# Scan differences as stick-breaking weights, and dilated blocks handled in pairs, in a two-layer hybrid attention trunk

## The chip, the cores and the metric

The kernel runs on one core of one Trainium2 chip. The metric is the device time of one execution in microseconds (us), lower is better. Three executions of the kernel before took 3222.48, 3223.91 and 3230.89 us, with a median of 3223.91 us. A core has several engines that run their own instruction streams side by side: TensorE (PE, matrix products and transposes; its weight loads are listed as PEld), VectorE (DVE), ScalarE (ACT), GpSimd (POOL) and SyncE (SP, which issues DMAs). They meet through semaphores.

## The reference, cut to what matters

Two layers, each with one input projection, two token mixers that read its outputs, SiLU gates, and one output projection. 2048 tokens, 4 stick-breaking heads and 12 dilated heads of 64 numbers each. Numbers are float32.

```python
# stick-breaking, for a block of 128 queries and the keys up to it
z = einsum('bhqd,bhkd->bhqk', qblk, k[:lk]) / 8
ls_z = log_sigmoid(z)
log_surv = where(mask, ls_z - z, 0)          # log(1 - sigmoid(z)), mask: key < query
acc = (sum of log_surv over the keys after this one)
a = where(mask, exp(ls_z + acc), 0)          # sigmoid(z[k]) * product over later keys of (1 - sigmoid(z))
o = einsum('bhqk,bhkd->bhqd', a, v[:lk])

# dilated window, three patterns (window, dilation): (128,1), (512,4), (2048,16)
# tokens r apart form a sequence; blocks of 128 queries see their own and the previous 128 keys
s = einsum('brnqhd,brnkhd->brnhqk', qb, kk) / 8     # kk: previous block and own block
# per pattern: softmax with its maximum and its sum; the three outputs are mixed by their denominators
```

## The kernel before, in words

A layer runs in three stretches: the projection with the gate path (until about 787 us in the first layer), the stick-breaking mixer `_stick` with the tail of the projection's stores (until about 1016 us), then the dilated mixer `_dilated`, whose last weights are interleaved with the output projection `_output` (until about 1613 us). The second layer repeats this. PE instructions of the mixers are pinned to the order in which the code issues them (`pin`); the other engines' orders are made by a scheduler when the program is built.

**Stick.** The work of a layer is 80 units: a pair of heads, a block of 128 queries, and up to 512 keys. `front(u)` makes the scores of both heads (two fp32r products per head, L541 and L542, and a mask product L544 in diagonal blocks), ACT takes sigmoid(-z) (L549, the survival factors g) and sigmoid(z) (L550), DVE runs a product scan over the keys (L551, into r, whose first entry carries over to the next unit of the block), and POOL multiplies sigmoid(z) by the scan (L557). `mid(u)` transposes the weights on PE (L570) and copies them out of PSUM (L572, ACT for head 0, DVE for head 1). `back(u)` makes the value products (L584). The loop issues `front(u+2)`, `mid(u)`, and after every second unit two `back`s in a row (`LEAD, BATCH = 2, 2`).

**Dilated.** Six pairs of heads, and for each 48 groups: 16 query blocks in each of the three patterns p = 0, 1, 2. A block has one key block if it is in pattern 0 (whose own and previous block share one window) or first in its sequence (4 of 16 in p = 1, 1 of 16 in p = 2), 21 of 48 in all; the others have two. `front(g)` makes four score products of 256 columns (L732: two heads, two halves of the precision split), also where only 128 columns are used; DVE adds the mask and takes the minimum (L734), ACT takes the exponential (L738). `mid(g)` transposes (L753, four or two times) and copies (L755, DVE for odd g, ACT for even g). Every fourth group `back` makes the value products of four groups (L767). The softmax statistics of a pair are brought together while the next pair runs: `stats_b` puts two sets of PE products (L802 to L807) into two banks of the ring `w_r`, ACT copies them (L810), and a chain of small DVE, POOL and ACT steps (L815 to L826, with a DVE reciprocal L822) makes the weights. `weigh` broadcasts the weights of one block with one PE product (L837) into a bank of `w_r`, and DVE multiplies the outputs by it (L838), 16 times per pair, one per group from the fifteenth group on. The last pair's weighs run in the tail, between output projection products (L932, L935, L936).

PSUM has eight banks: in `_dilated` the scores use 0, 1, 2, the transposes 3, 4, the value products 5, and `w_r` 6, 7. The loop issues one group per step: `front(g+3)`, `mid(g)`, every fourth step `back`, then statistics or one `weigh`.

Of the kernel before, what the change touches and what calls it, by code (L numbers as in the profile page):

```python
# [459 lines left out]
def _stick(tc, mem, sb_scr, g_scr, mix, ident, ident_r):  # L460
    nc = tc.nc
# [14 lines left out]
    wk1 = mem.get("G1", [128, 12, 512])  # L476
    r_s = Slices([wk0[:, i] for i in range(6)])
    gam = Slices([wk0[:, 6 + i] for i in range(6)])
    b_s = Slices([wk1[:, i] for i in range(6)])
    at_s = Slices([wk1[:, 6 + i] for i in range(6)])  # L480
    nc.gpsimd.memset(wk0[:, 6:12, 512:513], 1.0)
    qs_, ks1, ks2, vn, gt = {}, {}, {}, {}, {}
# [49 lines left out]
    def front(u):  # L532
# [14 lines left out]
        for h, z in enumerate(zs):  # L547
            b, g, r = b_s.get(), gam.get(), r_s.get()
            nc.scalar.activation(g[:, 512 - n:512], z[:, :n], AF.Sigmoid, scale=-0.125)  # L549
            nc.scalar.activation(b[:, :n], z[:, :n], AF.Sigmoid, scale=0.125)  # L550
            nc.vector.tensor_tensor_scan(  # L551
                out=r[:, 0:n + 1][:, ::-1], data0=g[:, 512 - n:513][:, ::-1],
                data1=z[:, 0:1].to_broadcast([128, n + 1]),
                initial=1.0 if top else carry[h][:, 0:1],
                op0=ALU.mult, op1=ALU.bypass)
            carry[h] = r
            nc.gpsimd.tensor_tensor(out=b[:, :n], in0=b[:, :n], in1=r[:, 1:n + 1], op=ALU.mult)  # L557
            prod[u].append(b)
# [4 lines left out]
    def mid(u):  # L563
        pr, i, lo, hi = units[u]
        n = hi - lo
        ats[u] = []
        for h, b in enumerate(prod.pop(u)):
            ps = t_r.get([128, 512])
            for j in range(n // 128):
                pin(nc.tensor.transpose(ps[:, 128 * j:128 * j + 128], b[:, 128 * j:128 * j + 128], ident))  # L570
            at = at_s.get()
            (nc.vector.tensor_copy if h else nc.scalar.copy)(at[:, :n], ps[:, :n])  # L572
            ats[u].append(at)
# [20 lines left out]
    todo = []  # L594
    LEAD, BATCH = 2, 2
    load(1)
# [20 lines left out]
def _dilated(tc, mem, v_scr, qk_scr, g_scr, mix, masks, sel, ident, neg1):  # L617
# [3 lines left out]
    nc.sync.dma_start(out=mk, in_=masks)  # L621
    s_r = mem.bank_ring(0, 1, 2)
    t_r = mem.bank_ring(3, 4)
    o_r = mem.bank_ring(5)
    w_r = mem.bank_ring(6, 7)
    pa, pb = mem.get("H0", [128, 2, 2, 256]), mem.get("H1", [128, 2, 2, 256])
    pe_s = Slices([pa[:, 0], pa[:, 1], pb[:, 0], pb[:, 1]])
    ta, tb = mem.get("H6", [128, 2, 2, 2, 128]), mem.get("H7", [128, 1024])
    td = mem.get("H5", [128, 2, 2, 2, 128])
    ts_s = Slices([td[:, 0], td[:, 1], ta[:, 0], ta[:, 1], tb[:, 0:512].rearrange("p (c h q) -> p c h q", c=2, h=2)])  # L630
# [74 lines left out]
    def front(g):  # L705
# [5 lines left out]
        c, n, first = geom(p, b)  # L711
        u0 = 0
        if p == 0:
            w0 = min(b, 14) * 128
            u0 = 128 * b - w0
        else:
            run, stp = (32, 4) if p == 1 else (8, 1)
            w0 = 0 if first else run * (n - 1)
        un = 128 if first else 256
        m0 = M_OWN[p] + 128 - un  # L720
        sc = s_r.get([128, 2, 256])
        pe = pe_s.get()
        for h in range(2):
            qb = qq[pr][h][p].bitcast(F32R)[:, 128 * b:128 * b + 128]
            for s in range(2):
                kt = kk[pr][h][s]
                if p == 0:
                    kv = kt[:, w0:w0 + 256]
                else:
                    kv = kt.rearrange("p (c a) -> p c a", c=NT)[  # L730
                        :, c::stp, w0:w0 + 2 * run].rearrange("p c (w a) -> p w c a", w=2)
                pin(nc.tensor.matmul(sc[:, h], qb, kv, start=s == 0, stop=s == 1))  # L732
        for h in range(2):
            nc.vector.tensor_tensor_reduce(  # L734
                out=pe[:, h, :un], in0=sc[:, h, u0:u0 + un], in1=mk[:, m0:m0 + un],
                scale=-0.125, scalar=3.0e38, op0=ALU.add, op1=ALU.min,
# [7 lines left out]
    def mid(g):  # L744
# [9 lines left out]
        ts = ts_s.get()  # L754
        (nc.vector.tensor_copy if g % 2 else nc.scalar.copy)(ts[:, :nch], tp[:, :nch])  # L755
        tss[g] = ts
# [39 lines left out]
    def stats_b(pr, eng):  # L796
# [15 lines left out]
        ll = sm[:, 1]  # L812
        mn = tb[0:32, 896:1024]
        ew = tb[0:32, 512:896].rearrange("p (q a) -> p q a", q=3)
        nc.vector.tensor_tensor(out=mn, in0=nm[:, 0], in1=nm[:, 1], op=ALU.min)  # L815
# [41 lines left out]
    for g in range(LEAD):  # L857
        front(g)
    for g in range(total):
        pr, t = g // 48, g % 48  # L860
# [4 lines left out]
        if pr + 1 < NPAIR:  # L865
# [4 lines left out]
            if t == 36:  # L870
                make_q(pr + 1, 1)
        if g + LEAD < total:
            front(g + LEAD)
        mid(g)
        if g % 4 == 0 and g:
            back(g - 4)
        if pr:
            if t == 1:
                stats_a(pr - 1, nc.gpsimd)
            elif t == 5:  # L880
                stats_b(pr - 1, nc.gpsimd)
            elif 15 <= t < 31:
                weigh(pr - 1, t - 15)
                if t % 4 == 2:
                    gate(pr - 1, (t - 15) // 4)
        yield
# [95 lines left out]
```

## Time and profile before

| | us |
|---|---|
| three executions | 3222.48, 3223.91, 3230.89 |
| median | 3223.91 |
| profiled execution | 3228.57 |
| its span on the core | 3226.8 |
| PE busy in it | 3137.9 (97%) |
| DVE busy | 1648.3 (51%) |
| ACT busy | 1534.4 (48%) |
| POOL busy | 1234.4 (38%) |

Busy times of PE overlap a little and their ends are modelled, since products are pipelined, so a PE that is 97% busy may still have gaps. The pace of PE is better read from the starts of successive groups of instructions in the timeline. The granted clock of PE was 0.99 to 1.00 of full speed (2.4 GHz) in all stretches shown below. The table hides that stages differ: in the projection PE alone is the limit, while in the mixers several engines take turns.

### The profile page before, as it was taken

Reading aid. Unit: us, or ns where it says so; the run is one execution under the profiler, and the core shown is the slowest. Engines: PE = TensorE matmul, PEld = TensorE weight load, DVE = VectorE, ACT = ScalarE, POOL = GpSimd, SP = SyncE. Lnnn points to the kernel's source line nnn. Section 1 sums busy time; section 2 is a strip of 40 time slices with the busy share of each in tenths; the row PEclk is TensorE's granted clock in tenths of the full one; section 3 lists DMA queues with packets and bytes.
Section 4 is the critical chain, followed back from the end, with each engine's and each line's share of the span. In section 5 each row is a group of like instructions: output and inputs, shape, how many; then the busy total and the mean of one; then the engine's idle time right before and its main releaser. Section 6 shows DMA issues by size and latency. Waiting matters only on the chain.

```text
span 3226.8 us, 59494 instructions
## 1 busy us (share of the span) xinstructions
PE 3137.9 (97%) x21968; PEld 2683.2 (83%) x21968; DVE 1648.3 (51%) x4147; ACT 1534.4 (48%) x4317; POOL 1234.4 (38%) x1302
## 2 busy tenths in 40 slices
PE   8999999999999999989999999999999999999899
PEld 8888888887777999878898888888877789988787
DVE  6134440015988777764141444301169887777721
ACT  5123331114878998962031233211158789988510
POOL 1067751102664444451010677511036734444500
PEclk9999999999999999999999999999999999999999
DMA  5123346317023556454442233463160235663443
GB/s 198 63 73 113 112 138 181 122 48 204 15 83 93 165 155 193 117 164 150 128 135 72 70 113 105 149 189 104 59 186 21 83 106 151 178 187 100 140 145 108
DMA packets 324066, 396.40 MB, mean 123 GB/s; under 512 B 20160, under 2 KB 270016, under 8 KB 313536
## 3 DMA queue, kind: packets, MB, share of 16 engines
q1 hardware_dynamic: 323776, 392.60, 40.0%
q8 instruction: 174, 2.85, 0.4%
q14 instruction: 116, 0.95, 0.1%
HBM read 235.24 MB, written 148.90 MB: 119 GB/s over the span
## 4 chain that ended last, share of the span: by engine, by line
PE 81%; DVE 5%; ACT 4%; POOL 4%; issue 3%; DMA 2%; SPq 0%; POOLq 0%; ACTq 0%; DVEq 0%
PE b L310 11%; PE b L311 11%; PE b L309 11%; PE b L732 7%; PE b L767 5%; PE b L753 5%; PE b L451 4%; PE b L453 4%; PE b L452 4%; PE b L935 4%; PE b L936 4%; PE b L932 3%; PE b L584 3%; PE b L367 2%; ACT H L738 2%
## 5 line engine op out<-in xcount | busy, mean ns | idle before, releaser
L738 ACT ACTIVATE H<-H,T 128x256 f32<-128x256 f32 (+1 forms) x1152 | 522.7, 457 | 45.9 <-DVE T L734 43.4
L311 PE MATMUL b<-F,F 128*128 128x512 f32 (+1 forms) x1344 | 484.1, 360 | 0.4 <-DVE F L282 0.3
L734 DVE CUSTOM_DVE_ANT_0 H<-b,M 128x256 f32<-128x256 f32 (+1 forms) x1152 | 368.6, 361 | 168.9 <-PE b L732 66.2
L732 PE MATMUL b<-F,F 128*128 128x256 f32 x2304 | 412.3, 303 | 0.3 <-DVE T L734 0.3
L557 POOL TENSOR_TENSOR G<-G,G 128x512 f32<-128x512 f32 (+3 forms) x320 | 320.5, 1017 | 228.5 <-DVE G L551 171.6
L551 DVE TENSOR_TENSOR_SCAN G<-G,b 128x513 f32<-128x513 f32 (+3 forms) x320 | 336.5, 1085 | 33.0 <-ACT G L550 32.7
L732 PEld LDWEIGHTS b<-F,F 128*128 128x128 f32 x2304 | 326.4, 190 | 20.1 <-issue 19.5
L310 PE MATMUL b<-F,G 128*128 128x512 f32 (+1 forms) x896 | 324.7, 362 | 0.0
L309 PE MATMUL b<-F,G 128*128 128x512 f32 (+1 forms) x896 | 324.3, 362 | 0.0
L310 PE MATMUL b<-F,F 128*128 128x512 f32 (+1 forms) x896 | 323.2, 361 | 0.0
L309 PE MATMUL b<-F,F 128*128 128x512 f32 (+1 forms) x896 | 321.9, 359 | 0.0
L753 PE MATMUL b<-ident,H 128*128 128x128 f32 x1800 | 292.9, 274 | 11.4 <-ACT H L755 5.5
L311 PEld LDWEIGHTS b<-F,F 128*128 128x128 f32 x1344 | 253.7, 189 | 38.4 <-DVE F L282 0.8
L135 POOL TENSOR_SCALAR U<-U 128x16 f32<-128x16 f32 (+1 forms) x80 | 33.7, 421 | 536.1 <-DVE U L334 315.5
L767 PE MATMUL b<-H,H 128*64 128x128 f32 x3600 | 229.8, 277 | 0.8 <-DVE H L755 0.8
L753 PEld LDWEIGHTS b<-ident,H 128*128 128x128 f32 x1800 | 215.6, 141 | 16.5 <-ACT H L755 8.6
L549 ACT ACTIVATE G<-b 128x512 f32<-128x512 f32 (+3 forms) x320 | 179.5, 563 | 103.6 <-PE b L542 87.8
L738 ACT ACTIVATION_READ_ACCUMULATOR H<-H,T 128x1 f32 x1152 | 219.3, 190 | 0.0
L767 PEld LDWEIGHTS b<-H,H 128*64 128x64 f32 x3600 | 193.8, 137 | 25.9 <-issue 23.4
L212 POOL TENSOR_TENSOR F<-H,F 128x1024 fp32r<-128x1024 f32 x22 | 53.9, 2456 | 380.7 <-ACT F L211 164.0
L333 ACT ACTIVATE H<-b 128x512 f32<-128x512 f32 x96 | 57.5, 600 | 294.8 <-PE b L311 293.8
L309 PEld LDWEIGHTS b<-F,G 128*128 128x128 f32 x896 | 168.9, 189 | 26.6
(165 smaller groups left out, 6844.2 us busy)
## 6 DMA issues: line engine op xcount, KB each, us to landing
qk_l<-H SPq DMA_DIRECT2D x192, 256.0 KB
F<-qk_l SPq DMA_DIRECT2D x48, 1024.0 KB
v_l<-S SPq DMA_DIRECT2D x288, 128.0 KB
H<-v_l SPq DMA_DIRECT2D x72, 512.0 KB
F<-qk_l SPq DMA_DIRECT2D x48, 512.0 KB
g_l<-S SPq DMA_DIRECT2D x64, 256.0 KB
G<-mixa_l SPq DMA_DIRECT2D x32, 448.0 KB
H<-in_w_in SPq DMA_DIRECT2D x24, 512.0 KB
```

Source lines behind the costliest of these rows:

```text
L309: nc.tensor.matmul(ps, hT(q, 0, k)[:, cs], wh, start=k == 0, stop=False)
L310: nc.tensor.matmul(ps, hT(q, 0, k)[:, cs], wl, start=False, stop=False)
L311: nc.tensor.matmul(ps, hT(q, 1, k)[:, cs], wh, start=False, stop=k == NK - 1)
L451: nc.tensor.matmul(ps, wh[:, k, w], hT(tq, 0, k), start=k == 0, stop=False)
L549: nc.scalar.activation(g[:, 512 - n:512], z[:, :n], AF.Sigmoid, scale=-0.125)
L551: nc.vector.tensor_tensor_scan(out=r[:, 0:n + 1][:, ::-1], data0=g[:, 512 - n:513][:, ::-1], data1=z[:, 0:1].to_broadcast([128, n + 1]), i ...
L557: nc.gpsimd.tensor_tensor(out=b[:, :n], in0=b[:, :n], in1=r[:, 1:n + 1], op=ALU.mult)
L732: pin(nc.tensor.matmul(sc[:, h], qb, kv, start=s == 0, stop=s == 1))
L734: nc.vector.tensor_tensor_reduce(out=pe[:, h, :un], in0=sc[:, h, u0:u0 + un], in1=mk[:, m0:m0 + un], scale=-0.125, scalar=3.0e38, op0=ALU. ...
L738: nc.scalar.activation(pe[:, h, :un], pe[:, h, :un], AF.Exp, scale=-1.0, bias=st[:, 0, p, h, b:b + 1], accum_out=st[:, 1, p, h, b:b + 1])
L753: pin(nc.tensor.transpose(tp[:, ch, h], pe[:, h, 128 * w:128 * w + 128], ident))
L767: pin(nc.tensor.matmul(ob[64 * h:64 * h + 64, b % 4], vq[(pr * 3 + p) * 2 + (b - ch) // 8][:, (b - ch) % 8, 64 * h:64 * h + 64], ts[:, ch, h],
```

## The change

In `_stick` the weight of a key is now the difference of two neighbouring entries of the scan, r[k+1] - r[k], made by POOL; the second sigmoid is gone. All copies of transposed weights are on ACT. Value products are issued for four units at a time. The rings change with it: r and g have 4 slots each instead of 6, the transposed weights 10 instead of 6.

In `_dilated` the scores of blocks with one key block are 128 columns wide instead of 256. Two groups are issued per step: eight score products, then (in the weigh part) one broadcast, then the value products if they are due, then the transposes of the first group, a second broadcast, and the transposes of the second group. Scores get bank 7, so `w_r` has bank 6 alone. DVE copies three of four groups, ACT one of four. Statistics are issued at step 2 and 6 and weighs at 18 to 33 (before: 1, 5, and 15 to 30). Some small buffers move.

```diff
-    r_s = Slices([wk0[:, i] for i in range(6)])
-    gam = Slices([wk0[:, 6 + i] for i in range(6)])
+    r_s = Slices([wk0[:, i] for i in range(4)])
+    gam = Slices([wk0[:, 4 + i] for i in range(4)])
     b_s = Slices([wk1[:, i] for i in range(6)])
-    at_s = Slices([wk1[:, 6 + i] for i in range(6)])
+    at_s = Slices([wk1[:, 6 + i] for i in range(6)] + [wk0[:, 8 + i, :512] for i in range(4)])
...
-            nc.scalar.activation(b[:, :n], z[:, :n], AF.Sigmoid, scale=0.125)
             nc.vector.tensor_tensor_scan(
...
-            nc.gpsimd.tensor_tensor(out=b[:, :n], in0=b[:, :n], in1=r[:, 1:n + 1], op=ALU.mult)
+            nc.gpsimd.tensor_tensor(out=b[:, :n], in0=r[:, 1:n + 1], in1=r[:, 0:n], op=ALU.subtract)
...
-            (nc.vector.tensor_copy if h else nc.scalar.copy)(at[:, :n], ps[:, :n])
+            nc.scalar.copy(at[:, :n], ps[:, :n])
...
-    LEAD, BATCH = 2, 2
+    LEAD, BATCH = 2, 4
...
-    s_r = mem.bank_ring(0, 1, 2)
+    s_r = mem.bank_ring(0, 1, 2, 7)
...
-    w_r = mem.bank_ring(6, 7)
+    w_r = mem.bank_ring(6)
...
-                    kv = kt[:, w0:w0 + 256]
+                    kv = kt[:, 128 * b:128 * b + 128]
...
-                        :, c::stp, w0:w0 + 2 * run].rearrange("p c (w a) -> p w c a", w=2)
-                pin(nc.tensor.matmul(sc[:, h], qb, kv, start=s == 0, stop=s == 1))
+                        :, c::stp, w0:w0 + run * un // 128].rearrange("p c (w a) -> p w c a", a=run)
+                pin(nc.tensor.matmul(sc[:, h, :un], qb, kv, start=s == 0, stop=s == 1))
...
-        (nc.vector.tensor_copy if g % 2 else nc.scalar.copy)(ts[:, :nch], tp[:, :nch])
+        (nc.scalar.copy if g % 4 == 1 else nc.vector.tensor_copy)(ts[:, :nch], tp[:, :nch])
...
-        if g + LEAD < total:
-            front(g + LEAD)
-        mid(g)
+        for u in (g + LEAD, g + LEAD + 1):
+            if u < total:
+                front(u)
+        if pr and 18 <= t < 34:
+            weigh(pr - 1, t - 18)
         if g % 4 == 0 and g:
             back(g - 4)
+        mid(g)
+        if pr and 18 <= t < 34:
+            weigh(pr - 1, t - 17)
+            if t % 4 == 0:
+                gate(pr - 1, (t - 18) // 4)
+        mid(g + 1)
         if pr:
-            if t == 1:
+            if t == 2:
                 stats_a(pr - 1, nc.gpsimd)
-            elif t == 5:
+            elif t == 6:
                 stats_b(pr - 1, nc.gpsimd)
-            elif 15 <= t < 31:
-                weigh(pr - 1, t - 15)
-                if t % 4 == 2:
-                    gate(pr - 1, (t - 15) // 4)
```

The orders below come from the two built programs. Line numbers of the changed kernel are a few lower: its scores are L727 (before L732), transposes L748 (L753), broadcast L832 (L837), its DVE product L833 (L838), the mask-and-minimum L729 (L734; on DVE each is two rows, the second a short read), the copies L750 (L755), the reciprocal L817 (L822). Names such as b_1350 are uses of PSUM banks, the other names are buffers.

PE in the weigh part of pair 2, one step of the kernel before and the next:

```order
L837 MATMUL b_1339_11265<-W_8008,F_996_8951 128x384
L732 MATMUL b_1340_11272<-F_1176_10186,F_1248_10637 128x256
L732 MATMUL b_1340_11272<-F_1177_10187,F_1248_10637 128x256
L732 MATMUL b_1340_11272<-F_1178_10191,F_1249_10642 128x256
L732 MATMUL b_1340_11272<-F_1179_10192,F_1249_10642 128x256
L753 MATMUL b_1341_11281<-ident,H_866_8003 128x128 x4
L837 MATMUL b_1343_11289<-W_8008,F_996_8951 128x384
```

The same place in the changed kernel, from the last score products of one step to the first of the next:

```order
L727 MATMUL b_1348_11180<-F_1177_10027,F_1249_10482 128x256
L832 MATMUL b_1350_11191<-W_7890,F_996_8791 128x384
L748 MATMUL b_1351_11194<-ident,H_866_7885 128x128 x4
L832 MATMUL b_1352_11200<-W_7890,F_996_8791 128x384
L748 MATMUL b_1353_11203<-ident,H_868_7887 128x128 x4
L727 MATMUL b_1356_11213<-F_1174_10021,F_1248_10477 128x256
```

Two broadcasts now stand four transposes apart, where four scores and four transposes stood between them; in every second step the value products stand between them too.

DVE at the same place in the changed kernel, with the product of the first broadcast behind the four minima of the step:

```order
L729 ISA H_865_7884,T_1271_10653<-b_1347_11171,M_7882 128x256
L729 ISA T_1271_10653 128x1
L729 ISA H_866_7885,T_1271_10653<-b_1348_11180,M_7882 128x256
L729 ISA T_1271_10653 128x1
L729 ISA H_866_7885,T_1271_10653<-b_1348_11180,M_7882 128x256
L729 ISA T_1271_10653 128x1
L833 TENSOR_TENSOR G_1121_9644<-G_1121_9644,b_1350_11191 128x3x128
L750 COPY H_867_7886<-b_1351_11194 128x512
L833 TENSOR_TENSOR G_1121_9644<-G_1121_9644,b_1352_11200 128x3x128
L750 COPY H_868_7887<-b_1353_11203 128x512
```

Before, two minima at most stood ahead of a product, and one copy in two was DVE's.

DVE between the last short step ahead of the reciprocal and the reciprocal itself, in the changed kernel:

```order
L811 TENSOR_TENSOR X_7889<-X_7889 32x128
L729 ISA H_866_7885,T_1271_10653<-b_1304_10903,M_7882 128x128
L729 ISA T_1271_10653 128x1
L729 ISA H_866_7885,T_1271_10653<-b_1304_10903,M_7882 128x128
L729 ISA T_1271_10653 128x1
L729 ISA H_866_7885,T_1271_10653<-b_1305_10912,M_7882 128x128
L729 ISA T_1271_10653 128x1
L729 ISA H_866_7885,T_1271_10653<-b_1305_10912,M_7882 128x128
L729 ISA T_1271_10653 128x1
L817 RECIPROCAL X_7889<-X_7889 32x128
L750 COPY H_868_7887<-b_1307_10931 128x256
```

Before, between L816 and L822, ten minima and two copies stood there in the statistics of pair 2.

## Rows read from the trace of the kernel before

**Rows 1.** Windows: stretch, length, busy PE, PEld, DVE, ACT, POOL (instructions), clock, DMA, GB/s.

```profile
787.00:1016.00 229.00, 213.63 (x2026) 172.48 (x2023) 209.05 (x256) 171.51 (x389) 155.53 (x161) 0.99 0.22 61
1162.00:1187.00 25.00, 23.32 (x235) 21.57 (x232) 21.31 (x88) 21.86 (x82) 14.38 (x16) 1.00 0.45 139
```

**Rows 2.** Groups by line, 787 to 1016 us: busy, mean ns, idle before and releasers.

```profile
L551 DVE TENSOR_TENSOR_SCAN G<-G,b 128x513 f32<-128x513 f32 (+3 forms) x152 | 158.6, 1077 | 16.2 <-ACT G L550 16.2
...
L570 PE MATMUL b<-ident,G 128*128 128x128 f32 x520 | 77.6, 278 | 9.5 <-ACT G L572 4.7 <-POOL G L557 3.7 <-ACT G L549 0.3
```

**Rows 3.** PE timeline in the stick: start, length, line, instructions.

```profile
928.00 1.97 PE L584 MATMUL b<-G,F 128*64 128x128 f32 x32
929.90 0.50 PE L541 MATMUL b<-F,F 128*128 128x512 f32 x1
...
930.92 1.03 PE L570 MATMUL b<-ident,G 128*128 128x128 f32 x8
931.71 0.36 PE L541 MATMUL b<-F 128*128 128x256 f32 x1
```

**Rows 4.** ACT timeline, the first sigmoid of those scores; in brackets its idle time.

```profile
930.66 0.60 ACT L549 ACTIVATE G<-b 128x512 f32<-128x512 f32 x1 [0.91 <-PE b L542]
```

**Rows 5.** DVE timeline, four scans in a row.

```profile
915.94 4.83 DVE L551 TENSOR_TENSOR_SCAN G<-G,b 128x513 f32<-128x513 f32 x4
```

**Rows 6.** POOL timeline, one weight product.

```profile
927.52 1.28 POOL L557 TENSOR_TENSOR G<-G,G 128x512 f32<-128x512 f32 x1 [2.33 <-PE b L570]
```

**Rows 7.** PE timeline in pattern 0 of the dilated mixer.

```profile
1143.35 0.72 PE L732 MATMUL b<-F,F 128*128 128x256 f32 x4
1143.90 0.60 PE L753 MATMUL b<-ident,H 128*128 128x128 f32 x4
1144.26 0.72 PE L732 MATMUL b<-F,F 128*128 128x256 f32 x4
```

**Rows 8.** PE timeline in the projection: sixteen fp32r transposes and what follows.

```profile
214.07 1.48 PE L367 MATMUL b<-ident_r,H 128*128 128x128 f32 x16
215.38 0.46 PE L310 MATMUL b<-F,G 128*128 128x512 f32 x1
```

**Rows 9.** Weight loads by line, whole span: busy, mean ns of one.

```profile
L732 PEld LDWEIGHTS b<-F,F 128*128 128x128 f32 x2304 | 326.4, 190 | 20.1 <-issue 19.5 <-PE b L732 0.7
...
L367 PEld LDWEIGHTS b<-ident_r,H 128*128 128x128 f32 x768 | 70.7, 140 | 6.3
```

**Rows 10.** Weigh part of pair 2, PE timeline: one broadcast.

```profile
1175.47 0.42 PE L837 MATMUL b<-W,F 128*128 128x384 f32 x1
```

**Rows 11.** The same place, DVE timeline: its product, and a minimum.

```profile
1176.45 0.55 DVE L838 TENSOR_TENSOR G<-G,b 128x384 f32<-128x384 f32 x1
1176.92 0.42 DVE L734 CUSTOM_DVE_ANT_0 H<-b,M 128x256 f32<-128x256 f32 x1
```

**Rows 12.** Broadcasts by line, whole span, PE: busy, mean ns, idle before and releasers.

```profile
L837 PE MATMUL b<-W,F 128*128 128x384 f32 x192 | 80.3, 418 | 10.3 <-POOL W L826 8.9 <-DVE G L838 1.1
```

**Rows 13.** Statistics of pair 2, PE timeline: second set, and a later wait.

```profile
1221.63 0.28 PE L802 MATMUL b<-ident,T 128*32 128x128 f32 x1
...
1225.44 0.44 PE L753 MATMUL b<-ident,H 128*128 128x128 f32 x2 [0.67 <-ACT H L755]
```

**Rows 14.** Statistics of pair 2, ACT timeline: copy of the first set.

```profile
1221.91 0.45 ACT L810 COPY X<-b 32x384 f32<-32x384 f32 x1
```

**Rows 15.** Statistics of pair 2, DVE timeline: last short step, and the reciprocal.

```profile
1222.78 0.28 DVE L816 TENSOR_TENSOR H<-H,X 32x128 f32<-32x128 f32 x1
...
1226.89 0.94 DVE L822 RECIPROCAL H<-H 32x128 f32<-32x128 f32 x1 [1.51 <-POOL H L821]
```

**Rows 16.** Tail of layer 1, PE timeline: two broadcasts.

```profile
1453.19 0.34 PE L837 MATMUL b<-W,F 128*128 128x384 f32 x1
...
1454.07 0.34 PE L837 MATMUL b<-W,F 128*128 128x384 f32 x1
```

**Rows 17.** The same place, DVE timeline: the product of the first.

```profile
1453.79 0.54 DVE L838 TENSOR_TENSOR G<-G,b 128x384 f32<-128x384 f32 x1
```

More of the change, by code (lines that the diff above doesn't have):

```diff
@@ L476, in _stick @@
     wk1 = mem.get("G1", [128, 12, 512])
-    r_s = Slices([wk0[:, i] for i in range(6)])
-    gam = Slices([wk0[:, 6 + i] for i in range(6)])
+    r_s = Slices([wk0[:, i] for i in range(4)])
+    gam = Slices([wk0[:, 4 + i] for i in range(4)])
     b_s = Slices([wk1[:, i] for i in range(6)])
-    at_s = Slices([wk1[:, 6 + i] for i in range(6)])
-    nc.gpsimd.memset(wk0[:, 6:12, 512:513], 1.0)
+    at_s = Slices([wk1[:, 6 + i] for i in range(6)] + [wk0[:, 8 + i, :512] for i in range(4)])
+    nc.gpsimd.memset(wk0[:, 4:8, 512:513], 1.0)
     qs_, ks1, ks2, vn, gt = {}, {}, {}, {}, {}
@@ L621, in _dilated @@
     nc.sync.dma_start(out=mk, in_=masks)
-    s_r = mem.bank_ring(0, 1, 2)
+    s_r = mem.bank_ring(0, 1, 2, 7)
     t_r = mem.bank_ring(3, 4)
     o_r = mem.bank_ring(5)
-    w_r = mem.bank_ring(6, 7)
+    w_r = mem.bank_ring(6)
     pa, pb = mem.get("H0", [128, 2, 2, 256]), mem.get("H1", [128, 2, 2, 256])
-    pe_s = Slices([pa[:, 0], pa[:, 1], pb[:, 0], pb[:, 1]])
     ta, tb = mem.get("H6", [128, 2, 2, 2, 128]), mem.get("H7", [128, 1024])
+    pe_s = Slices([pa[:, 0], pa[:, 1], pb[:, 0], pb[:, 1], tb[:, 512:1024].rearrange("p (h k) -> p h k", h=2)])
     td = mem.get("H5", [128, 2, 2, 2, 128])
@@ L711, in front @@
         c, n, first = geom(p, b)
[L712 to L716, printed above, removed]
+        un = 128 if first else 256
+        if p:
             run, stp = (32, 4) if p == 1 else (8, 1)
             w0 = 0 if first else run * (n - 1)
-        un = 128 if first else 256
         m0 = M_OWN[p] + 128 - un
@@ L727, in front @@
                 if p == 0:
-                    kv = kt[:, w0:w0 + 256]
+                    kv = kt[:, 128 * b:128 * b + 128]
                 else:
                     kv = kt.rearrange("p (c a) -> p c a", c=NT)[
-                        :, c::stp, w0:w0 + 2 * run].rearrange("p c (w a) -> p w c a", w=2)
-                pin(nc.tensor.matmul(sc[:, h], qb, kv, start=s == 0, stop=s == 1))
+                        :, c::stp, w0:w0 + run * un // 128].rearrange("p c (w a) -> p w c a", a=run)
+                pin(nc.tensor.matmul(sc[:, h, :un], qb, kv, start=s == 0, stop=s == 1))
         for h in range(2):
             nc.vector.tensor_tensor_reduce(
-                out=pe[:, h, :un], in0=sc[:, h, u0:u0 + un], in1=mk[:, m0:m0 + un],
+                out=pe[:, h, :un], in0=sc[:, h, :un], in1=mk[:, m0:m0 + un],
                 scale=-0.125, scalar=3.0e38, op0=ALU.add, op1=ALU.min,
@@ L812, in stats_b @@
         ll = sm[:, 1]
-        mn = tb[0:32, 896:1024]
-        ew = tb[0:32, 512:896].rearrange("p (q a) -> p q a", q=3)
+        mn = xa[0:32, 768:896]
+        ew = nm
         nc.vector.tensor_tensor(out=mn, in0=nm[:, 0], in1=nm[:, 1], op=ALU.min)
@@ L858, in _dilated @@
         front(g)
-    for g in range(total):
+    for g in range(0, total, 2):
         pr, t = g // 48, g % 48
```

## The prediction

> **What bounds the kernel now.** I read the windows first, then the groups by line, then the timelines. The window of the stick stage is 229 us long, PE is busy for 213.63 of them and DVE for 209.05 [rows 1]; the reader is to see that neither has the stage to itself. PE's own pace there comes from its starts: two full units' value products take 1.90 us (32 instructions, 0.059 each), four scores 1.02, eight transposes 0.79 [rows 3], so a full unit costs PE 0.95 + 1.02 + 0.79 = 2.76 us. The window has 520 transposes, or 65 full units, and 76 units' scans [rows 2]: 65 x 2.76 = 179 us, eleven more fronts at up to 1.02, and some 5 for the transposes that prepare keys, make about 195. That is an estimate; 34 us are PE's gaps, of which the rows name 9.5 at the transposes and, on DVE, 16.2 of waiting for the second sigmoid [rows 2].
>
> The dilated stage is PE's in pattern 0 (groups follow each other every 0.91 us without a gap) [rows 7]. In pattern 1, with the weighs in it, PE has 23.32 of 25.00 us and DVE 21.31 [rows 1]: a delay on DVE's side there reaches PE soon.
>
> **The change part by part**, per layer; I double at the end.
>
> *Stick, -9.* Removing a sigmoid per head frees ACT, moving half the copies frees DVE. So PE's 34 us of gaps become reachable, but not all of them. Follow a unit's chain: scores start at 929.90 [rows 3], the first sigmoid at 930.66 and takes 0.60 [rows 4], two scans take 1.20 each (4.83 for four) [rows 5], the difference on POOL 1.28 [rows 6]: 0.76 + 0.60 + 2.4 + 1.28 = 5.0 us until the second head's weights can be transposed. PE reaches these transposes after two rounds of scores and transposes and one more head's four, 2 x 1.81 + 0.4 = 4.0 us. With value products after every second unit, 1.9 us stand between and cover the missing 1.0. With four units at a time, two units in four have 3.8 us between and the other two nothing; the second of those inherits the slack that the first one's wait makes. So one wait of 1.0 per four units: 20 x 1.0 = 20 us come back. All copies on ACT double the 4.7 that transposes wait for ACT's copies [rows 2]: +4.7. So -34 + 20 + 4.7 = -9. The bounds are 0 (the waits move from the sigmoid to POOL and ACT) and -34. POOL's instruction count is the same, and its operand ranges are as long. The rings of four slots hold two units, which is what the lead of two needs; at no cost, covered by the scan being a unit behind.
>
> *128-column scores, -4.5.* 504 products per layer are narrowed (1008 of 2304). Four take 0.72 with the single one at 0.36 (the 256-column product in [rows 3]): (0.72 - 0.36) / 3 = 0.12 apart [rows 3, 7]. No row shows an fp32r product below 256 columns. The nearest are the projection's fp32r transposes of 128 columns, sixteen in 1.31 us, 82 ns each [rows 8]. But their weight loads take 140 ns and the score products' loads 190 [rows 9], and a narrow product still loads all its weights. Scaled by that, 82 x 190 / 140 = 111 ns. I take this value, nearest to the products themselves: 504 x 9 ns = 4.5 us saved. Bounds: 82 ns (-19) and no gain; a price above the wide product's is a rival below. DVE's minima on these groups are as wide as before.
>
> The Trainium skill ("TensorE: Matmul & The Clock Gate", section "LDWEIGHTS (loading the stationary operand)") says that a weight load takes its number of columns divided by 1.2 in ns, 107 for 128 columns, however narrow the product. The transposes at 82 ns [rows 8] come faster than that, so the trace does not bear it out for them; for the scores it is close to the 111. By it the term would be -6.5 and by the transposes' pace -19.
>
> *Two groups per step, -2.* Of the 0.55 that four scores take from start to the transposes, 4 x 0.12 are theirs, so 0.07 is the change from transposes to scores [rows 7]; half of 288 such changes go, -10. But eight transposes in a row take 0.79 where two times four take 0.72 [rows 3, 7], which gives most of it back. Bounds -10 and 0.
>
> *Copies from ACT to DVE, 0.* A quarter of 288 copies, 72 per layer, change over. Between the patterns DVE has room; in pattern 1 four more of some 0.6 us make 23.7 of 25 [rows 1]. What hides them is PE's work there; if DVE becomes the limit they cost 4 x 0.6 x 5 pairs = 12.
>
> *One bank for the broadcasts, +20.* The second broadcast of a step waits until DVE has multiplied by the first. In the steps without value products PE has only the broadcast (384 columns, 0.16 at the full clock) and four transposes (0.36) in between [rows 7], 0.52. From the start of a broadcast to the end of its product the trace shows 1175.47 to 1177.00, 1.53 us [rows 10, 11]. So PE stands for 1.0, with all scores and transposes of the next step queued behind it: four such steps in a pair, five pairs, 20 us. The steps with value products have 1.9 more in between and wait for nothing. Bounds: a product that starts almost at once needs 1.14 (1453.19 to 1454.33, [rows 16, 17]), a stall of 0.6, +12; two more minima ahead of the product on DVE add 0.84 [rows 11], +37. Later weighs (twelve groups after the statistics instead of ten) take away the wait for POOL's weights, 8.9 over both layers [rows 12]: -3, with nothing else late next.
>
> *Statistics, +9.* The second set of products waits in the one bank for ACT's copy of the first, which ends at 1222.36 [rows 14] where the set began at 1221.63 [rows 13]: 0.73 for each of six pairs. Then the reciprocal. From the last short DVE step to it the chain through POOL and ACT takes 1222.78 to 1226.89, 4.11 us, and it takes 0.87 [rows 15]. DVE's order now puts four to eight minima into that time, where six to ten and a copy or two stood, and the copies that free the transposes' banks come behind. PE's work meanwhile is the second set (thirteen instructions, about 1.0), eight narrow scores 0.9, value products 0.95, four transposes 0.36, eight more scores 0.9: 4.1 us from the first copy's end, while the copy behind the reciprocal ends 0.42 + 4.11 + 0.87 + 0.3 = 5.7 after it. PE waits 1.6, where 0.67 stood before [rows 13]. So 5 x (0.73 + 1.6 - 0.67) + 0.73 = 9. Bounds 0 (DVE has work in hand from the step before) and 15.
>
> *Tail, +5.5.* Sixteen broadcasts per layer, 0.88 us apart at the closest [rows 16], need 1.14 in one bank, some more where another DVE product stands ahead [rows 17]: 16 x 0.35 = 5.5. Bounds 0 and 10.
>
> **The sum.** -9 - 4.5 - 2 + 0 + 20 - 3 + 9 + 5.5 = +16 per layer, +32 for two. The profiled execution took 3228.6 us, so 3260.6 by it; it lies 4.7 above the median, so **3256** us by the median, 1.0% slower. Its own range, from weighs at +12 to +37 and copies up to +12, is some 3235 to 3300.
>
> **Rivals.**
> 1. *The stick reaches PE's floor* (other side: not slower). If the scans keep a unit in hand, so that the 5.0 us of the chain fall to below 4.0, the 20 us do not come back and the copies on ACT are early: -34 in place of -9, -50 in all, 3206. For it: ACT loses a third of its stick work and DVE its copies, so queues ahead of sigmoid and scan vanish. Against it: the 5.0 us above have no queue in them. It decides at a wait of under 0.5 us for the transposes in the units without value products between.
> 2. *Narrow scores at the transposes' pace*, 82 ns: 504 x 29 ns = 14.5 more per layer, 3227, no change. For it: sixteen transposes do run so [rows 8]. Against: the loads of 190 ns [rows 9].
> 3. *A narrow fp32r product runs in passes like an f32 product.* The value products show two instructions for each f32 product, 0.059 apiece, for a stationary of 64 columns [rows 3]; four such for 128 columns make 0.237. That is 504 x 0.126 = +63 per layer, less some 9 of stalls that it covers: about 3365. For it: both kernels pad the stick's short scores to 256, so no row excludes it. Against it: the fp32r transposes are single instructions at 82 ns.
> 4. *The change's waits are half of what I take* (weighs at +10, statistics at +3): so -16 per layer and 3224, no change. It decides by how much DVE has in hand when the second broadcast is due.
>
> **How the numbers follow.** A measurement of this kernel tells about 0.3% from no change, that is 3214 to 3234. Chances: the forecast 0.42 (slower), rival 1 0.14 (0.12 faster, 0.02 same), rival 2 0.18 (0.05 faster, 0.10 same, 0.03 slower), rival 3 0.18 (slower), rival 4 0.08 (0.05 same, 0.03 slower). So faster 0.17, same 0.17, slower 0.66. The range 3203 to 3310 leaves out rival 3 and the lower end of rival 1, about 2 in 10.
>
> **What would show each step.** In the profile of the changed kernel: narrow scores 0.11 apart in pattern 0, so that a pair of groups takes 1.7 us or more; broadcasts with some 20 us per layer of idle time released by DVE's product; a wait of 1 to 2 us at the transposes behind the reciprocal; a stick window of about 220 us with POOL's differences as the releaser of transposes. Wrong would be: narrow scores near 0.08 or above 0.2, a stick window near 195, or broadcasts that hardly wait.

## The result, and the profile after

The changed kernel took 3259.03 us (median of four executions, 3255.29 to 3264.10) beside 3223.19 us for the kernel before: a ratio of 1.0107, with a 95% interval of 1.0086 to 1.0128. The forecast was 3256 us.

Where the time went, from the starts of PE's instructions in both traces (us; the first number of each pair is the kernel before):

| stretch | layer 1 | layer 2 |
|---|---|---|
| first stick score to last value product | 250.6, 236.6 | 250.2, 237.4 |
| first to last dilated score | 396.3, 416.3 | 399.4, 415.9 |
| of it pair 0 | 59.7, 56.8 | 59.7, 56.6 |
| of it pairs 1 to 5, mean | 67.3, 71.9 | 67.9, 71.8 |
| last dilated score to next layer's stick, or to the end | 957.4, 968.1 | 207.5, 214.4 |

So the stick stage gave back 13.4 us per layer, the dilated stage cost 18.3 and the tail behind it 8.8. In the dilated stages PE was busy for 384.0 and 383.3 us, 4 to 5 less than before (387.7 and 388.8), and stood for 32, where it stood for 9 to 11 before: the loss there is waiting. Two windows of the kernel after (columns as in rows 1) answer to [rows 1]: the stick stage, and a stretch of pair 2.

```profile
787.00:1001.00 214.00, 203.65 (x2004) 169.85 (x2002) 165.38 (x173) 140.96 (x309) 138.20 (x157) 0.98 0.22 61
1162.00:1187.00 25.00, 21.93 (x226) 19.69 (x226) 20.77 (x80) 17.79 (x64) 13.58 (x16) 1.00 0.35 117
```

DVE's and ACT's busy time in the stick stage fell by 44 and 31 us, and PE has 10 us left that it is not busy. In the weigh part no engine is at its limit, and yet the pairs take longer: the mark of a wait that goes round from engine to engine. The groups of PE by line, whole span of the kernel after, show it in the idle time and its releasers:

```profile
L748 PE MATMUL b<-ident,H 128*128 128x128 f32 x1800 | 273.8, 279 | 18.6 <-ACT H L750 9.3 <-DVE H L750 8.7
...
L569 PE MATMUL b<-ident,G 128*128 128x128 f32 x1088 | 156.7, 278 | 5.5 <-POOL G L556 4.7
...
L832 PE MATMUL b<-W,F 128*128 128x384 f32 x192 | 75.8, 395 | 42.0 <-DVE G L833 42.0
...
L797 PE MATMUL b<-ident,T 128*32 128x128 f32 x24 | 6.8, 284 | 12.3 <-ACT X L805 12.3
```

The broadcast L832 answers to [rows 12]: it waited 1.1 us for DVE's product before and waits 42.0 now; the 8.9 for POOL's weights are gone. L797 is the first product of a set of statistics. One wait of the broadcast, in PE's timeline of the kernel after:

```profile
1172.86 0.34 PE L832 MATMUL b<-W,F 128*128 128x384 f32 x1
1173.04 0.60 PE L748 MATMUL b<-ident,H 128*128 128x128 f32 x4
1174.68 0.45 PE L832 MATMUL b<-W,F 128*128 128x384 f32 x1 [1.05 <-DVE G L833]
```

and what DVE did meanwhile:

```profile
1173.04 0.42 DVE L729 CUSTOM_DVE_ANT_0 H<-b,M 128x256 f32<-128x256 f32 x1
...
1173.38 0.42 DVE L729 CUSTOM_DVE_ANT_0 H<-b,M 128x256 f32<-128x256 f32 x1
...
1173.73 0.42 DVE L729 CUSTOM_DVE_ANT_0 H<-b,M 128x256 f32<-128x256 f32 x1
1174.07 0.08 DVE L729 DVE_READ_ACCUMULATOR2_ANT T<- 128x1 f32 x1
1174.07 0.55 DVE L833 TENSOR_TENSOR G<-G,b 128x384 f32<-128x384 f32 x1
```

The first broadcast of the step started at 1172.86. DVE was still at the step's minima, so its product (L833) ended at 1174.62, and the second broadcast started at 1174.68. PE had transposes for about half a microsecond in between and then stood for 1.05.

### The profile page after: what moved, and what is told of

Same layout as the page of the kernel before. It is cut to its first block, busy times and chain, and to the rows that moved or that the text cites. A ratio compares the mean times of both kernels' runs of the same rounds, so it can differ in the third digit from the quotient of the medians.

```text
span 3253.6 us, 59277 instructions
## 1 busy us (share of the span) xinstructions
PE 3118.7 (96%) x21968; PEld 2665.9 (82%) x21968; DVE 1620.1 (50%) x4131; ACT 1428.6 (44%) x4013; POOL 1202.9 (37%) x1302
## 3 DMA queue, kind: packets, MB, share of 16 engines
q8 instruction: 174, 2.85, 0.4%
## 5 line engine op out<-in xcount | busy, mean ns | idle before, releaser
L729 DVE CUSTOM_DVE_ANT_0 H<-b,M 128x256 f32<-128x256 f32 (+1 forms) x1152 | 352.6, 361 | 62.7 <-PE b L727 36.5
L556 POOL TENSOR_TENSOR G<-G 128x512 f32<-128x512 f32 (+3 forms) x320 | 291.5, 922 | 233.1 <-DVE G L550 192.9
L550 DVE TENSOR_TENSOR_SCAN G<-G,b 128x513 f32<-128x513 f32 (+3 forms) x320 | 326.0, 1079 | 76.7 <-ACT G L549 66.1
L727 PE MATMUL b<-F,F 128*128 128x256 f32 (+1 forms) x2304 | 340.2, 292 | 0.0
L727 PEld LDWEIGHTS b<-F,F 128*128 128x128 f32 x2304 | 295.5, 192 | 2.3 <-issue 2.3
L748 PE MATMUL b<-ident,H 128*128 128x128 f32 x1800 | 273.8, 279 | 18.6 <-ACT H L750 9.3
L311 PEld LDWEIGHTS b<-F,F 128*128 128x128 f32 x1344 | 253.7, 189 | 37.8 <-DVE F L282 0.3
L750 DVE COPY H<-b 128x512 f32<-128x512 f32 (+1 forms) x432 | 233.0, 558 | 101.2 <-PE b L748 101.1
L748 PEld LDWEIGHTS b<-ident,H 128*128 128x128 f32 x1800 | 202.8, 141 | 54.5 <-issue 25.0
L549 ACT ACTIVATE G<-b 128x512 f32<-128x512 f32 (+3 forms) x320 | 163.3, 558 | 124.1 <-PE b L542 105.9
L931 PE MATMUL b<-F,H 128*128 128x512 f32 x448 | 181.5, 405 | 11.9 <-ACT F L915 10.8
```

The costliest lines, as they stand in the source:

```text
L311: nc.tensor.matmul(ps, hT(q, 1, k)[:, cs], wh, start=False, stop=k == NK - 1)
L550: nc.vector.tensor_tensor_scan(out=r[:, 0:n + 1][:, ::-1], data0=g[:, 512 - n:513][:, ::-1], data1=z[:, 0:1].to_broadcast([128, n + 1]), i ...
L556: nc.gpsimd.tensor_tensor(out=b[:, :n], in0=r[:, 1:n + 1], in1=r[:, 0:n], op=ALU.subtract)
L727: pin(nc.tensor.matmul(sc[:, h, :un], qb, kv, start=s == 0, stop=s == 1))
L729: nc.vector.tensor_tensor_reduce(out=pe[:, h, :un], in0=sc[:, h, :un], in1=mk[:, m0:m0 + un], scale=-0.125, scalar=3.0e38, op0=ALU.add, op ...
L748: pin(nc.tensor.transpose(tp[:, ch, h], pe[:, h, 128 * w:128 * w + 128], ident))
```

## The experiments

Each run was timed beside the kernel before on the same chip. Ratios are to that, with 95% intervals in brackets.

### The halves of the change

e1 takes the stick's half of the diff alone, e2 the dilated half alone.

> The kernel before with the change of the stick mixer alone. In the two traces the stick stage got shorter by 14.0 us in layer 1 and 12.8 us in layer 2. Theory (the two halves of the change act apart): 3223 - 27 = 3196 us. Rival (a shorter stick stage only moves the wait to the loads of the dilated stage, so part of the gain is lost there): 3205 us or more, with a longer first pair in the dilated stage.

Measured: 3201.91 us beside 3228.35, 0.9918 [0.9902, 0.9935], 26 us faster where 27 were expected. The stick stage took 239.4 and 236.9 us, the dilated stage 399.4 and 397.8 (396.3 and 399.4 in the kernel before), its first pair 59.7 and 60.0 (59.7 twice). The half acts by itself.

> The kernel before with the change of the dilated mixer alone. Theory (the halves act apart): the dilated stage is longer by 20.0 and 16.5 us and its tail by 10.7 and 6.9 us, together 54, so 3277 us. Rival (part of the loss comes from the new stick stage, whose work runs into the dilated one): 3265 us or less.

Measured: 3294.32 us beside 3228.35, 1.0206 [1.0191, 1.0222], 66 us slower; broadcasts waited 41.5 us for DVE, where it was 42.0 with both halves. The sum of the halves, -26 + 66, is the whole change's 36 within the intervals. In the profiled execution some of the 12 us beyond the 54 goes with the clock: windows from the dilated stage's start show

```profile
1014.00:1018.00 4.00, 3.89 (x33) 3.46 (x32) 3.63 (x23) 3.29 (x16) 0.00 (x0) 1.00 0.71 215
1018.00:1022.00 4.00, 2.85 (x18) 2.49 (x19) 2.31 (x17) 3.79 (x20) 0.00 (x0) 0.73 0.81 309
1022.00:1026.00 4.00, 4.00 (x29) 3.67 (x26) 1.22 (x9) 2.13 (x9) 0.00 (x0) 0.50 0.31 84
```

The third number from the end is PE's granted clock: in a stretch in which PE was busy for 2.85 of 4 us, behind a wait of 1.15 us, it went to 0.50 (1.2 GHz), and pattern 0 of the first pair took 20.9 us there, beside 14.2 in the whole change. The whole change has a wait of 1.15 us at the same place, and its clock stayed at 1.00 there, so the wait alone does not tell why it fell.

### Four units at a time

e4 is e1 with value products for two units at a time.

```diff
-    LEAD, BATCH = 2, 4
+    LEAD, BATCH = 2, 2
```

> As the first of these runs, but with value products issued for two units at a time, as before. Theory (the gain of the stick stage comes from the sigmoid and the copies that are gone, and four units at a time bring little): within 6 us of it. Rival 1 (the longer bursts pay, since PE changes between kinds of products less often): slower than it by 10 us or more. Rival 2 (by the prediction's chain of 5.0 us against 4.0, the longer bursts cost a wait of 1.0 us per four units): faster than it by 20 us or more.

Measured: 3198.33 us, 0.9911 [0.9896, 0.9925]; by the medians 3.6 us faster than e1, which the intervals do not tell from none. The wait that the prediction described is there, but small. Transposes of the stick and second score products by line, first e1, then e4:

```profile
L569 PE MATMUL b<-ident,G 128*128 128x128 f32 x1088 | 158.1, 280 | 5.1 <-POOL G L556 4.3
L542 PE MATMUL b<-H,F 128*128 128x512 f32 (+2 forms) x320 | 118.9, 372 | 12.7 <-DMA H<-F 12.7
```

```profile
L569 PE MATMUL b<-ident,G 128*128 128x128 f32 x1088 | 152.7, 278 | 0.7 <-POOL G L556 0.3
L542 PE MATMUL b<-H,F 128*128 128x512 f32 (+2 forms) x320 | 119.3, 373 | 23.0 <-DMA H<-F 23.0
```

Four units at a time cost 4.4 us of waits at the transposes in both layers together, and 3.9 more at scores that wait for DVE's scan (none in e4), not 40. The times hardly show it, since e4 waits 10.3 us longer for a DMA, the one that L542's keys come from. So the gain of the stick is that of the sigmoid, the copies and the rings together; no run takes these apart.

### The one bank

e3 gives broadcasts two banks again, e5 also weighs later, and e10 weighs later with the one bank.

```diff
-    s_r = mem.bank_ring(0, 1, 2, 7)
+    s_r = mem.bank_ring(0, 1, 2)
-    w_r = mem.bank_ring(6)
+    w_r = mem.bank_ring(6, 7)
...
-        if pr and 18 <= t < 34:
-            weigh(pr - 1, t - 18)
+        if pr and 24 <= t < 40:
+            weigh(pr - 1, t - 24)
...
```

> The changed kernel with broadcasts in banks 6 and 7 and scores in 0, 1, 2, as before. Theory (the one bank makes the waits): the 42.0 us of waits of broadcasts for DVE's product and most of the 12.3 us at the statistics go, so about 3259 - 50 = 3209 us, if three score banks do for two groups per step. Rival (DVE is the limit in the weigh part, because of its copies and the order of two groups): the waits move to the transposes and the time falls by 10 us at most, to 3249 us or more.

Measured: 3258.44 us, 1.0096 [1.0081, 1.0111]: no faster, and the theory looked refuted. But the trace shows another wait in the old one's place, and not the one at the transposes that the rival named, by line:

```profile
L832 PE MATMUL b<-W,F 128*128 128x384 f32 x192 | 80.3, 418 | 54.1 <-POOL W L821 52.9 <-DVE G L833 1.0
```

Broadcasts no longer wait for DVE, but once per pair for the weights. POOL's, DVE's and PE's timelines of pair 2 name what was late:

```profile
1154.37 0.45 POOL L816 TENSOR_TENSOR X<-X 32x128 f32<-32x128 f32 x1
1161.36 0.98 POOL L818 TENSOR_TENSOR X<-X 32x384 f32<-32x384 f32 x1 [6.54 <-DVE X L817]
```

```profile
1160.34 0.94 DVE L817 RECIPROCAL X<-X 32x128 f32<-32x128 f32 x1
```

```profile
1164.57 0.69 PE L832 MATMUL b<-W,F 128*128 128x384 f32 x1 [5.28 <-POOL W L821]
```

The reciprocal L817 could start at 1154.82. DVE started it at 1160.34: the scheduler had made a new order for the new banks and put 24 minima and 7 copies between L811 and it, where the changed kernel has four to eight minima and at most two copies. PE waited 5.28 us for the weights, and the clock fell to 0.50 during the wait (1161.6 to 1168.4):

```profile
1160.00:1167.00 7.00, 2.43 (x11) 2.28 (x11) 2.68 (x8) 2.17 (x9) 2.95 (x4) 0.61 0.52 192
```

> As the changed kernel with two banks for the broadcasts, and the weighs at steps 24 to 39 instead of 18 to 33, so that the weights can be ready in spite of the late reciprocal. Theory (the one bank cost 20.6 us per layer, and in the run with two banks a late reciprocal put a wait for POOL's weights of 26.5 us per layer in its place): without both about 3258 - 50 = 3208 us. Rival (DVE is the limit of the weigh part): 3240 us or more, with the waits at transposes or broadcasts in another place.

Measured: 3205.83 us, 0.9936 [0.9914, 0.9957]. The same place of the step in e5's PE timeline:

```profile
1176.82 0.34 PE L832 MATMUL b<-W,F 128*128 128x384 f32 x1
1177.00 0.60 PE L748 MATMUL b<-ident,H 128*128 128x128 f32 x4
1177.36 0.42 PE L832 MATMUL b<-W,F 128*128 128x384 f32 x1
1177.62 0.60 PE L748 MATMUL b<-ident,H 128*128 128x128 f32 x4
```

The second broadcast follows 0.54 us behind the first, and all waits of broadcasts together are 1.3 us. The reciprocal is as late as in e3 in six of ten pairs; with the later weighs nothing waits for it.

> The changed kernel with its one bank and the weighs at steps 24 to 39: the control to the run with two banks and late weighs. Theory (the second bank made the gain there, the later weighs only made the weights ready): within 8 us of the changed kernel, 3259, with broadcasts waiting some 20 us per layer for DVE. Rival (the later place alone frees the weigh part): 3235 us or less.

Measured: 3278.09 us beside 3224.57, 1.0167 [1.0152, 1.0182]. The broadcasts waited 42.0 us, as expected, so the later place frees nothing; what was not expected is that it costs some 19 us more than the changed kernel. The dilated stages (419.4 and 422.9 us) hold about half of that, the tails (976.1 and 217.0 us) the rest. Against this control the second bank is worth 2.3%, 72 us. In pairs 1 to 4 pattern 1 takes 20.5 to 20.7 us beside 21.8 to 23.5, and pattern 2, with more of the weighs, about 25 beside 28.4. The two runs differ in the rings of banks and in the order that the scheduler made for them.

> The kernel before, one group per step, with bank 6 alone for broadcasts and statistics. Theory: a broadcast comes every 1.1 us there and needs 1.04 to 2.25 us to the end of its product, 1.6 in the mean, so 80 x 0.4 = 32 us of waits per layer, 4 at the statistics and 3 in the tail, at most 78 in all, about 3290 us. Rival (the bank hardly matters, since DVE and PE make up for a wait in the next step): under 20 us.

```diff
-    w_r = mem.bank_ring(6, 7)
+    w_r = mem.bank_ring(6)
```

Measured, on the kernel before: 3257.82 us beside 3227.61, 1.0097 [1.0080, 1.0114], 30 us slower; both sides of the expectation missed. Its broadcasts and statistics:

```profile
L802 PE MATMUL b<-ident,T 128*32 128x128 f32 x24 | 6.7, 279 | 8.9 <-ACT X L810 8.9
```

```profile
L837 PE MATMUL b<-W,F 128*128 128x384 f32 x192 | 82.6, 430 | 18.7 <-DVE G L838 11.2 <-POOL W L826 7.3
```

11.2 us of waiting, not 64. The time from a broadcast to the end of its product is no constant: its median in the loop fell from 1.53 us in the kernel before to 1.10 here. That DVE works off what stood ahead of the product while PE waits is the likely reason, but no run isolates it. The new waits at broadcasts and statistics are some 17 of the 30 us; the rest is not traced.

### Other orders

e6 puts the second broadcast behind the second group's transposes; e9 copies in turn.

```diff
-        if pr and 18 <= t < 34:
-            weigh(pr - 1, t - 17)
...
         mid(g + 1)
+        if pr and 18 <= t < 34:
+            weigh(pr - 1, t - 17)
...
```

> The changed kernel with its one bank, the second broadcast of a step behind the second group's transposes. Theory (the wait is the time from a broadcast to the end of its product, less the PE work in between): four more transposes, 0.36 to 0.4 us, in the steps without value products, so the waits of broadcasts fall from 20.6 to some 13 us per layer and the time by 15 us to about 3244. Rival (DVE's backlog): the waits go to transposes and the time stays within 5 us of the changed kernel.

Measured: 3267.63 us, 1.0126 [1.0109, 1.0143], not faster than the changed kernel. Broadcasts waited 10 us less, transposes 5 more:

```profile
L748 PE MATMUL b<-ident,H 128*128 128x128 f32 x1800 | 263.0, 280 | 23.7 <-ACT H L750 11.6 <-DVE H L750 11.5
...
L832 PE MATMUL b<-W,F 128*128 128x384 f32 x192 | 78.5, 409 | 32.2 <-DVE G L833 31.5
```

Both sides of the expectation missed. The second broadcast of a step waits less, but only eight scores stand between it and the first one of the next step, which now waits too: 77 waits for DVE instead of 42. These waits still sum to 5 us less than in the changed kernel without the time showing it: in the dilated stages PE is busy for 390.5 us per layer instead of 384. Why its work takes longer there is open.

```diff
-        (nc.scalar.copy if g % 4 == 1 else nc.vector.tensor_copy)(ts[:, :nch], tp[:, :nch])
+        (nc.vector.tensor_copy if g % 2 else nc.scalar.copy)(ts[:, :nch], tp[:, :nch])
```

> The changed kernel with the copies of transposed weights on DVE and ACT in turn, as before, instead of three of four on DVE. Theory (the copies lie beside PE's work, the one bank makes the waits): within 6 us of the changed kernel, 3259, broadcasts still waiting 15 us per layer or more. Rival (DVE's load makes the products late): 15 us faster or more, broadcasts waiting under 10 us per layer.

Measured: 3268.00 us, 1.0141 [1.0125, 1.0156], by the medians 9 us slower than the changed kernel, 3 more than the theory allowed. Broadcasts waited 39.5 us; transposes waited for ACT's copies 20.6 us, where it was 9.3. DVE's load of copies is not what makes the products late, and three copies of four on DVE are, if anything, a gain in this order.

### Narrow scores, and the parts put together

e7 is the kernel before with 128-column scores.

```diff
...
-                pin(nc.tensor.matmul(sc[:, h], qb, kv, start=s == 0, stop=s == 1))
+                pin(nc.tensor.matmul(sc[:, h, :un], qb, kv, start=s == 0, stop=s == 1))
...
```

> The kernel before with 128-column scores where there is one key block, and nothing else. In the changed kernel narrow products follow each other every 0.112 us, wide contiguous ones every 0.119 and strided ones every 0.120 to 0.137. Theory: 504 products per layer by some 8 ns make 4 us per layer, 8 us in all, 0.25%. Rival (the narrow products also free the changes between kinds of products and the transfers from PSUM): 20 us or more.

Measured: 3214.26 us, 0.9962 [0.9947, 0.9977], 0.38% or some 12 us faster; the expected 0.25% lies in the interval.

> The stick mixer without the second sigmoid and with value products for two units at a time, and 128-column scores in the order of before with two banks for broadcasts. Theory (the parts add up): 0.9911 x 0.9962 = 0.9873 of the kernel before, about 3183 us. Rival (the gains overlap): 3195 us or more.

Measured: 3189.24 us beside 3224.57, 0.9898 [0.9882, 0.9915], between the two expectations: faster than both kernels of this study, with the narrow scores' part smaller than alone (e4 had 0.9911), though the intervals overlap.

> The same stick mixer with two groups per step, two banks for broadcasts and late weighs. Theory (two groups per step save changes between scores and transposes, but the output's tail is longer, as in the run with two banks and late weighs): 3202 us, slower than one group per step by 15 to 20 us. Rival (pairs pay): 3185 us or less.

Measured: 3202.65 us, 0.9935 [0.9920, 0.9950], 13 us slower than e11, and so on the theory's side. In its dilated stage, 388.2 and 387.9 us, it is 3 us shorter per layer than e11 (391.1, 390.8), in the tails (967.6, 214.9 beside 956.3, 207.5) 11 and 7 longer.

## Why the prediction was right, point by point

By stage the sum holds: the dilated terms make +19.5 per layer and 18.3 was measured, the stick -9 and -13.4, the tail +5.5 and 8.8. What follows asks which terms hold for their own reason.

**One bank, +20: right in place and cause, somewhat small.** In layer 1's loop the broadcasts waited 20.6 us [rows 10, 11 gave the 1.53 us], at 20 places, 1.05 at the one shown where 1.0 was worked out for the steps without value products. That idle time counts from modelled ends. By starts, which the prediction reckoned with, the two broadcasts of such a step are 1.82 us apart (median of 40) and 0.53 in e5, so PE loses 1.28 each, some 25 per layer: with four minima ahead of it the product ends 1.76 us after its broadcast's start, not 1.53. e5 against its control e10 shows the bank as the cause; e9 excludes DVE's copies. The price belongs to this order of PE: e8 has one bank in the order of before, and its broadcasts wait for DVE 5.3 us per layer in the loop. The step that held only by luck of the order is that nothing else is late next: e3 shows a wait of the same size right behind.

**Narrow scores, -4.5: right in price, small in effect.** The median distance of narrow products in pattern 0 is 0.112 us in the kernel after, where 0.111 was forecast from the weight loads [rows 8, 9], and of the wide ones there in the kernel before 0.119. A narrow group in PE's timeline of the kernel after, and what follows:

```profile
1150.70 1.09 PE L727 MATMUL b<-F,F 128*128 128x128 f32 x8
1151.71 1.09 PE L762 MATMUL b<-H,H 128*64 128x128 f32 x16
1152.74 0.66 PE L748 MATMUL b<-ident,H 128*128 128x128 f32 x4
1153.15 1.20 PE L727 MATMUL b<-F,F 128*128 128x256 f32 x8
1154.19 0.69 PE L748 MATMUL b<-ident,H 128*128 128x128 f32 x4
```

Eight narrow products take 1.01 us, eight wide ones 1.04: half the columns save 3%. Neither the transposes' 82 ns nor four passes came. The Trainium skill ("TensorE: Matmul & The Clock Gate", section "LDWEIGHTS (loading the stationary operand)") gives 107 ns for the load of 128 columns. The 0.112 lies near it, but the loads themselves take 190 ns each in the trace [rows 9], so no row here shows that they set the pace.

**Stick, -9: right in sum, wrong in its terms.** Measured -13.4. The 34 us of gaps were too many: PE is busy for 213.63 of the 229 us in [rows 1], which leaves 15. In e4, whose transposes wait 0.7 us in both layers, the stage takes 235 of 250 us, and 11.5 of the 235 are waits for a DMA (5.7 before). So 15 us per layer came, and by an estimate from e4 without these waits 27 at most were to be had. The wait of 1.0 us in each four units, 20 us per layer, is 2.2 at the transposes and 2.0 at the scores in e1 and e4's difference. The 4.7 for ACT's copies did not come: the stick's transposes in the kernel after wait 5.5 us in both layers, 4.7 of them for POOL. The step that failed is the chain of 5.0 us against 4.0: it took a start with empty hands for every four units, and PE waited for POOL's differences 13 times in both layers, 0.36 us in the mean, not 40 times 1.0. That scans and differences work ahead during the 3.5 us of a value burst is the likely reason; no run isolates it. Two errors of some 20 us cancelled, which is luck.

**Statistics, +9: right in kind.** PE's timeline of pair 2 in the kernel after, at the second set and behind the reciprocal:

```profile
1144.51 0.28 PE L797 MATMUL b<-ident,T 128*32 128x128 f32 x1 [0.84 <-ACT X L805]
...
1150.28 0.66 PE L748 MATMUL b<-ident,H 128*128 128x128 f32 x4 [1.18 <-DVE H L750]
```

0.84 and 1.18, where 0.73 and 1.6 were forecast. The 0.84 is the longest of its kind in the loop; the others are 0.56 to 0.68, and the two sets in the tails wait 2.11 and 4.25. The 1.18 comes behind seven of ten reciprocals, and as long a wait stood behind three of ten in the kernel before; the term counts 1.6 behind all and 0.67 there before. Over the whole span the sets waited 12.3 us (8.8 forecast), transposes 7 us more than before (9 forecast), some 5 of them behind reciprocals. In the kernel before six minima and one copy stand ahead of the reciprocal of [rows 15]; the ten and two named with the change stand ahead of the one before it.

**Tail, +5.5: measured 8.8, with a second cause that was put at nothing.** Broadcasts are 1.09 us apart instead of 0.87 in the tail, nine times at most, some 2 us, and the second set waits as above. e3, the kernel after with two banks, has neither, and its tails (964.4 and 212.1 us) are only 3.7 and 2.3 us shorter: the rest comes without the one bank. There PE waits 21.9 us for the output's weights in both layers, 13.3 in the kernel before and 15.3 in the kernel after, where the second set's waits stand ahead of them. The buffers into which these weights are loaded lie in the page that holds the outputs of the even pairs (G0), which the last weigh and gate of pair 4 free; weighs at 18 to 33 free it later than 15 to 30 did. PE waits by line in the tail of layer 1, first before (1412 to 1613 us), then after (1417.6 to 1629):

```profile
L935 PE MATMUL b<-F,H 128*128 128x512 f32 x217 | 87.0, 401 | 3.4 <-POOL F L917 3.4
L932 PE MATMUL b<-F,H 128*128 128x512 f32 x217 | 87.0, 401 | 3.6 <-ACT F L916 3.6
```

```profile
L931 PE MATMUL b<-F,H 128*128 128x512 f32 x217 | 88.3, 407 | 7.8 <-ACT F L915 6.9 <-DVE G L955 0.9
L934 PE MATMUL b<-F,H 128*128 128x512 f32 x217 | 88.0, 406 | 1.7 <-POOL F L916 1.7
L935 PE MATMUL b<-F,H 128*128 128x512 f32 x216 | 87.3, 405 | 2.5 <-DVE H L926 2.5
```

12.0 us of waits for operands of the output instead of 7.0, of which 8.6 are for the weights (ACT's L915, POOL's L916), and 2.1 at the second set. Later weighs lengthen the tail with one bank (e10) as with two (e5: 970.6 and 215.2 us, with 25.9 us of waits for the weights); that the page is what they wait for is read from the code, and no run moved the buffers to show it. A stretch of the tail's first 28 us, before and after, has the clock at 0.82 and 0.74:

```profile
1412.00:1440.00 28.00, 19.85 (x140) 13.95 (x140) 13.02 (x24) 16.05 (x37) 17.82 (x16) 0.82 0.62 206
```

```profile
1417.00:1445.00 28.00, 17.55 (x129) 13.12 (x128) 14.88 (x23) 12.67 (x25) 14.77 (x14) 0.74 0.69 227
```

PE is busy for less of it, and the clock is lower, so the stretch loses more than its waits.

**Two per step (-2) and copies (0)** cannot be told apart from the rest; e12's dilated stage is 3 us per layer shorter than e11's with both in it, and with later weighs too. **Later weighs, -3**: the wait for POOL's weights is gone, as forecast (8.9 over both layers is 4.5 per layer, of which the sum took 3 without a reason), but its price in the tail was not seen.

**The rivals.** The stick did not reach the rival's floor, which is 216 us in the table's measure (250 less 34): e4 takes 235, and without its waits for a DMA 224 by the estimate above. The transposes' pace and the four passes are excluded by the 0.112. Halved waits did not come.

## What to carry to other kernels

When two users of a PSUM bank stand closer together on PE than the time from a product to the end of its reading, the difference is paid at every pair of them; read that time from the trace, with what stands ahead of the reader on its engine, and expect it to shrink once the writer waits. A moved step is also a moved end of a buffer's life: ask which later load takes the same memory. Before a verdict on an experiment that frees a resource, look whether the scheduler has made another order with it: e3 was as slow as the changed kernel for a wholly different reason. And two equal times need not mean that a wait was nothing: in e4 another wait had grown in its place.

## What the runs showed of the hardware

An fp32r product of 128 columns is hardly cheaper than one of 256: 0.112 against 0.119 us apart, with weight loads of 190 ns, where fp32r transposes of the same shape load in 140 ns and run 0.082 apart [rows 8, 9]. And the granted clock can fall for longer than the wait ahead of it: a wait of 5.28 us in e3 went with 0.50 from 1161.6 to 1168.4 us, while one of 1.15 us in e2 was followed by 20 us at 0.50, and pattern 0 took 6.7 us longer there than in the kernel after, where a wait of the same length left the clock at 1.00.
